# Placing the first pair of the next feed-forward quarter ahead of this quarter's second product, and beginning that product with its B11 block

## The chip, the cores and the metric

The kernel runs on one core of a Trainium2 chip. The metric is device time in microseconds (us) of the whole kernel, from launch to end, as the median of several runs. A profiled execution of the same program gives the trace; its own time is given beside its span.

The engines that matter here are TensorE (PE in the profile; PEld is its weight load), VectorE (DVE), ScalarE (ACT), GpSimd (POOL, which here issues the accumulating DMAs) and SyncE (SP, which issues the plain ones).

## What is computed

The reference is a decoder trunk of two layers on 512 tokens and 16 meta tokens, with a model width of 1024. Each layer runs a mixer of three head groups, a layer norm, a squared-ReLU feed-forward block of width 4096, and a second layer norm. Only the feed-forward block is touched by the change:

```python
def squared_relu_mlp(h, w1, w2):
    return jnp.square(jax.nn.relu(h @ w1)) @ w2
...
    for l in range(DEPTH):
        mix = hybrid_mixer(h, w_in[l], mla_q_norm[l], mla_kv_norm[l], w_uq[l], w_ukv[l], w_out[l], pos, valid)
        h = layer_norm(DN_ALPHA * h + mix, ln1_g[l], ln1_b[l])
        h = layer_norm(DN_ALPHA * h + squared_relu_mlp(h, w_ff1[l], w_ff2[l]), ln2_g[l], ln2_b[l])
```

## The kernel before

**Precision.** Every float32 operand is split into a high part and a low part, `hi` by a cast on ScalarE and `lo` by a subtraction on VectorE. Each product is three matmuls (hi·hi, hi·lo, lo·hi).

**Tiling.** Activations lie transposed, features on partitions and tokens along the free dimension. The feed-forward width of 4096 is cut into four quarters of 1024 (`qd` 0 to 3). In a quarter the first product (`h @ w1`, function `ff1_pair`) makes eight 128-row tiles, two at a time, as four pairs (`i` 0 to 3). The second product (`... @ w2`, function `ff2_pair`) reads that quarter's eight tiles and adds to the eight output tiles `r`, again two at a time, as four pairs (`m` 0 to 3). In quarter 0 three of the four pairs of the first product are made without the block scheme (`ff1`); in quarter 3 two of the four pairs of the second product are (`ff2`).

**Strassen pairs.** A pair is one step of Strassen's scheme in Winograd's form: `strassen` makes seven block products of half the tokens each (264 columns in layer 0, 256 in layer 1). They go by the names `x1` (A11 by B11), `z1` (S1 by T1), `z2` (S4 by B22), `x2` (S2 by T2), `y` (A12 by B21), `x3` (S3 by T3) and `x4` (A22 by T4). With four contraction tiles and three matmuls each, a block product has 12 matmuls and a pair 84. The products sum up in three PSUM banks: X collects x1, x2, x3 and x4, Z collects z1 and z2, Y holds y. After each product a function of the dictionary `done` reads the bank (in a second product: VectorE adds it to a half of `r`), and the next product into that bank has to wait for this read.

**What VectorE has to do.** A pair's weights come by five plain loads and two accumulating ones (`strassen_weights`). VectorE adds two sums and subtracts seven low parts, nine instructions of 512 columns. In a first-product pair it also makes the block sums B and T of the squared ReLU and their low parts: three instructions of 512 or 528 columns and eight of 256 or 264 (nine in quarter 3). In a second-product pair it does the seven additions to `r`, of 256 or 264 columns.

**Buffers.** The pools are `U` (75 tiles of 528 columns, activations), `W` (14 tiles, split weights, as many as one pair needs), `R` (8 tiles, raw weights) and 8 PSUM banks.

**What sets the order.** `record` writes every instruction down in program order, and `Recorder.schedule` (line 312) then puts them in order with a cost model of its own: each engine takes the instruction that can start first by the model, and of equals the one with the lower rank, then the one written first (lines 347 and 350). All pairs of a layer's feed-forward block have one rank (line 1418), so the order in which the loops call `ff1_pair` and `ff2_pair` decides among them. A matmul of a later pair is put ahead wherever the model sees the next product not ready. On the chip each engine then takes its own list strictly as it stands.

Of the kernel before, what the change touches and what calls it, by code (L numbers as in the profile page):

```python
# [225 lines left out]
class Recorder:  # L226
# [13 lines left out]
    def add(self, eng, fn, args, kw):  # L240
        op = Op()
        op.i, op.eng, op.fn, op.args, op.kw = len(self.ops), eng, fn, args, kw
        op.prio = (self.cur, op.i)
        ins, outs = [], []
        named = [("", a) for a in args] + list(kw.items())
        for n, (k, v) in enumerate(named):
            if isinstance(v, View):
                is_out = k in ("out", "accum_out") or (n == 0 and k == "")
                (outs if is_out else ins).append(v)
        deps = set()  # L250
        op.tiles = []
        for w, vs in ((False, ins), (True, outs)):
            for v in vs:
                box = v.box()
                t = v.t
                if t.cls.name == "ps":
                    box = (0, P, 0, 1 << 30)
                if t not in op.tiles:
                    op.tiles.append(t)
                keep = []  # L260
                for (o, ow, b) in t.hist:
                    hit = b[0] < box[1] and box[0] < b[1] and b[2] < box[3] and box[2] < b[3]
                    if hit and (w or ow) and o is not op:
                        deps.add(o)
                    covered = w and box[0] <= b[0] and b[1] <= box[1] and box[2] <= b[2] and b[3] <= box[3]
                    if not (covered and o is not op):
                        keep.append((o, ow, b))
                keep.append((op, w, box))
                t.hist = keep
        for t in op.tiles:  # L270
            t.left += 1
        op.deps = deps
        op.users = []
        self._cost(op, ins, outs)
        self.ops.append(op)
        return op
# [149 lines left out]
class Builder:  # L426
# [176 lines left out]
    def parts(self, d, H):  # L603
        def run(x, names, hi=None, lo=None):
            n = H * len(names)
            if hi is None:
                hi, lo = self.unit(F32R)[:, :n], self.unit(F32R)[:, :n]
            self.split(hi, lo, x[:, :n], "a")
            for j, k in enumerate(names):
                d[k] = (hi[:, j * H:j * H + H], lo[:, j * H:j * H + H])  # L610
            return hi, lo
        return run
# [734 lines left out]
    def layer(self, l, h, first):  # L1347
# [74 lines left out]
        H = NQ // 2  # L1422
        us, xs, hs = [[] for _ in range(4)], {}, []
# [15 lines left out]
        def ff1_pair(qd, i):  # L1439
            w = self.strassen_weights(self.a["wff1"][l, 8 * qd + i], self.a["wff1"][l, 8 * qd + i + 4])  # L1440
            z1 = self.unit()[:, :H]
            A, B = slice(0, H), slice(H, 2 * H)
            sub, stt = nc.vector.tensor_sub, nc.vector.scalar_tensor_tensor
            d = {}
            parts = self.parts(d, H)

            def square(x, scale, src):
                nc.scalar.activation(x, src, AF.Relu, scale=scale)
                nc.scalar.activation(x, x, AF.Square)


            p, q, t, m = (self.unit() for _ in range(4))
            b11, b12, b21, b22 = p[:, A], m[:, A], t[:, A], q[:, A]
            t1, t2, t3, t4 = p[:, B], m[:, B], q[:, B], t[:, B]
            if qd == 3:
                b12, b22, t1, t3 = p[:, B], t[:, B], m[:, A], q[:, B]
                t4 = q[:, A]
            if i % 2 == 0:
                self.half = [(self.unit(F32R), self.unit(F32R)) for _ in range(2 if qd == 3 else 1)]
            o = B if i % 2 else A  # L1460

            def x1(X, Y, Z):
                nc.vector.tensor_add(b11, X, b11)
                square(b11, 1.0, b11)

            def x2(X, Y, Z):
                nc.vector.tensor_add(b12, X, b12)
                square(b12, 1.0, b12)
                sub(t1, b11, b12)
                if qd == 3:  # L1470
                    parts(t1, ("t1",), *(x[:, o] for x in self.half[1]))
                    d["plain"] = [parts(p, ("b11", "b12"))]
                else:
                    parts(p, ("b11", "t1"))

            def x3(X, Y, Z):
                nc.vector.tensor_add(b22, X, z1)
                square(b22, -1.0, b22)
                sub(t3, b22, b12)
                stt(out=t2, in0=t3, scalar=-1.0, in1=b11, op0=ALU.mult, op1=ALU.subtract)  # L1480
                parts(t2, ("t2",), *(x[:, o] for x in self.half[0]))
                if qd < 3:
                    parts(q, ("b22", "t3"))

            def x4(X, Y, Z):
                square(b21, -1.0, X)
                stt(out=t4, in0=t2, scalar=-1.0, in1=b21, op0=ALU.mult, op1=ALU.subtract)
                if qd == 3:
                    d["plain"].append(parts(t, ("b21", "b22")))
                    parts(q, ("t4", "t3"))  # L1490
                else:
                    parts(t, ("b21", "t4"))
            self.strassen(w, hs, ("z1", "y", "x1", "z2", "x2", "x3", "x4"), H, dict(
                z1=lambda X, Y, Z: nc.scalar.copy(z1, Z), y=lambda X, Y, Z: nc.scalar.copy(b11, Y),
                z2=lambda X, Y, Z: nc.scalar.copy(b12, Z), x1=x1, x2=x2, x3=x3, x4=x4))
            us[qd].append(d)

        def ff2_pair(qd, m):
            w = self.strassen_weights(self.a["wff2"][l, qd, 2 * m], self.a["wff2"][l, qd, 2 * m + 1])

            def add(row, col, op=ALU.add):
                def run(ps):
                    mt, c = 2 * m + row, slice(col * H, col * H + H)
                    o = r[mt][:, c]
                    if (mt, col) not in touched:
                        touched.add((mt, col))
                        nc.vector.scalar_tensor_tensor(out=o, in0=o, scalar=ALPHA, in1=ps, op0=ALU.mult, op1=op)
                    else:
                        nc.vector.tensor_tensor(o, o, ps, op=op)
                return run  # L1510
            sub = ALU.subtract
            self.strassen(w, us[qd], ("z1", "x1", "z2", "x2", "y", "x3", "x4"), H, dict(
                z1=lambda X, Y, Z: add(1, 1, sub)(Z), x1=lambda X, Y, Z: add(0, 0)(X), z2=lambda X, Y, Z: add(0, 1)(Z),
                x2=lambda X, Y, Z: add(0, 1)(X), y=lambda X, Y, Z: add(0, 0)(Y), x3=lambda X, Y, Z: add(1, 1, sub)(X),
                x4=lambda X, Y, Z: add(1, 0, sub)(X)))

# [39 lines left out]
            us[0].append(self.strassen_inputs(xs[i][1][:, :NQ], xs[i + 4][1][:, :NQ], H, i))  # L1556
        for i in range(npl, 4):
            ff1_pair(0, i)
        for m in range(4):
            ff2_pair(0, m)  # L1560
        for qd in range(1, 4):
            for i in range(4):
                ff1_pair(qd, i)
            for m in range(4 if qd < 3 else 4 - nf // 2):
                ff2_pair(qd, m)
        plain = [u["plain"][0] for u in us[3]] + [u["plain"][1] for u in us[3]]
        final = l == DEPTH - 1
        ws = {mt: self.wload(self.a["wff2"][l, 3, mt]) for mt in range(8 - nf, 8)}
# [174 lines left out]
```

## Time and profile before

| | before |
|---|---|
| median of 3 runs | 1547.27 us (1546.6 to 1547.67) |
| the profiled execution's own time | 1546.99 us |
| its span | 1545.2 us |
| PE busy | 1504.6 us, 97% of the span |
| DVE busy | 1303.8 us, 84% |
| ACT busy | 963.7 us, 62% |
| share of the chain that ended last: PE, DVE, ACT | 87%, 9%, 2% |

The feed-forward blocks lie at about 480 to 770 us (layer 0) and 1229 to 1510 us (layer 1) of the span. All matmuls of a helper stand under one line of the program (L414), so stretches of time, not lines, tell the stages apart. A group of rows "PE ... x672" in the timeline is a run of matmuls without an idle gap between them; the bracket behind a row gives the idle time ahead of it and whose signal ended that time.

### The profile page before, as it was taken

The page shows a single profiled execution, that of the slowest core. Times are in us where ns is not written, and L with a number is a line of the kernel's source. Part 1 is how long each engine was busy: PE and PEld are TensorE (multiplying, and loading weights), DVE is VectorE, ACT ScalarE, POOL GpSimd, SP SyncE. Part 2 cuts the span into 40 slices and gives each one's busy share as a digit, 9 for nine tenths or more (in the row PEclk, how much of TensorE's full clock was granted, in tenths as well). Part 3 has the DMA queues.
Part 4 walks back from the last instruction along what each step waited for, and adds up shares of the span by engine and source line. Part 5 has one row for each costly group of instructions (what it writes and reads, how often), then busy time and mean ns, then how long its engine had stood idle before and what let it go on. Part 6 is the DMA issues. An engine that isn't in the chain of part 4 may idle for free.

```text
span 1545.2 us, 31629 instructions
## 1 busy us (share of the span) xinstructions
PE 1504.6 (97%) x11490; PEld 1443.6 (93%) x11490; DVE 1303.8 (84%) x3131; ACT 963.7 (62%) x2263; POOL 197.9 (13%) x309
## 2 busy tenths in 40 slices
PE   6999999999999999999999999999999999999997
PEld 6999999988999999999999999888889899999996
DVE  7778877998789898888877778779987988989896
ACT  5675744578667484757646657446884857666670
POOL 4113100010001111111102112001000011111110
PEclk9999999999999999999999999999999999999999
DMA  5424412321124767677514333424212277777752
GB/s 196 117 78 124 141 62 76 100 81 49 56 83 115 185 165 178 177 181 175 171 56 131 103 91 95 127 76 125 57 62 83 69 190 180 186 183 181 186 154 82
DMA packets 102668, 190.32 MB, mean 123 GB/s; under 512 B 13552, under 2 KB 14832, under 8 KB 102512
## 3 DMA queue, kind: packets, MB, share of 16 engines
q1 hardware_dynamic: 81840, 145.98, 30.0%
q0 software_dynamic: 20672, 42.32, 14.9%
q8 instruction: 90, 1.47, 0.4%
q14 instruction: 66, 0.54, 0.1%
HBM read 167.87 MB, written 2.10 MB: 110 GB/s over the span
## 4 chain that ended last, share of the span: by engine, by line
PE 87%; DVE 9%; ACT 2%; issue 1%; DMA 0%; SPq 0%; DVEq 0%; ACTq 0%
PE ps L414 87%; DVE u L414 6%; ACT u L414 2%; DVE t L414 2%; DVE w L414 1%; DMA u<-in_xm 0%; SPq L414 0%; DVE r L414 0%; ACT w L414 0%; DVEq L1738 0%; ACT t L414 0%; DVEq L414 0%; ACTq L414 0%
## 5 line engine op out<-in xcount | busy, mean ns | idle before, releaser
L414 PE MATMUL ps<-u,w 128*128 128x256 f32 (+3 forms) x9384 | 1281.2, 294 | 14.7 <-DVE u L414 7.6
L414 PEld LDWEIGHTS ps<-u,w 128*128 128x128 f32 x9384 | 1199.7, 189 | 49.7 <-DVE u L414 11.3
L414 ACT CAST w<-r 128x512 fp32r<-128x512 f32 x610 | 364.5, 617 | 293.0 <-PE ps L414 249.2
L414 DVE TENSOR_TENSOR w<-r,w 128x512 fp32r<-128x512 f32 x604 | 404.8, 686 | 59.2 <-ACT w L414 42.9
L414 DVE TENSOR_TENSOR u<-u,u 128x512 fp32r<-128x512 f32 (+10 forms) x541 | 283.3, 548 | 10.8 <-ACT u L414 8.9
L414 DVE TENSOR_TENSOR u<-ps,u 128x256 fp32r<-128x256 f32 (+11 forms) x518 | 198.0, 409 | 48.3 <-ACT u L414 28.8
L414 PE MATMUL ps<-u,u 128*128 128x272 f32 (+5 forms) x1012 | 183.8, 307 | 1.7 <-ACT u L414 0.9
L414 POOL DMA_DIRECT2D r<-in_wff x108 | 94.8, 881 | 652.0 <-DVE u L414 331.4
L414 ACT CAST u<-u 128x512 fp32r<-128x512 f32 (+7 forms) x287 | 149.8, 540 | 39.9 <-DVE u L414 34.7
L414 ACT ACTIVATE u<-u 128x256 f32<-128x256 f32 (+5 forms) x349 | 161.7, 475 | 15.3 <-DVE u L414 12.3
L414 PEld LDWEIGHTS ps<-u,u 128*128 128x128 f32 (+1 forms) x1012 | 150.2, 190 | 8.6 <-ACT u L414 1.4
L414 ACT ACTIVATE u<-ps 128x512 f32<-128x512 f32 (+9 forms) x185 | 88.6, 484 | 89.8 <-PE ps L414 78.6
L414 DVE TENSOR_TENSOR u<-u,ps 128x256 f32<-128x256 f32 (+3 forms) x236 | 98.7, 429 | 43.6 <-PE ps L414 42.3
L414 POOL DMA_DIRECT2D u<-u x112 | 58.0, 523 | 483.7 <-ACT u L414 442.6
L414 PE MATMUL ps<-ident,u 128*128 128x128 f32 x672 | 103.4, 278 | 12.4 <-DVE t L414 9.2
L414 ACT COPY u<-ps 128x256 f32<-128x256 f32 (+6 forms) x186 | 72.1, 395 | 54.3 <-PE ps L414 52.2
L414 PEld LDWEIGHTS ps<-ident,u 128*128 128x128 f32 x672 | 79.7, 142 | 19.1 <-DVE t L414 7.9
L414 ACT CAST u<-ps 128x16 fp32r<-128x16 f32 (+7 forms) x260 | 72.4, 330 | 26.4 <-PE ps L414 15.8
L414 DVE TENSOR_TENSOR r<-r,r 128x512 f32<-128x512 f32 x108 | 74.0, 685 | 2.3 <-DMA r<-in_wff 2.1
L414 DVE SCALAR_TENSOR_TENSOR u<-ps,u 128x512 f32<-128x512 f32 (+7 forms) x73 | 41.6, 579 | 25.5 <-ACT u L414 23.2
L414 ACT ACTIVATE u<-ps,t 128x512 f32<-128x512 f32 (+4 forms) x86 | 48.0, 561 | 16.7 <-DVE t L414 13.5
L414 DVE CAST u<-u 128x256 fp32r<-128x256 f32 (+5 forms) x147 | 49.6, 353 | 8.2 <-ACT u L414 7.7
(57 smaller groups left out, 600.6 us busy)
## 6 DMA issues: line engine op xcount, KB each, us to landing
r<-in_wff SPq DMA_DIRECT2D x310, 256.0 KB, 3.3
r<-in_win SPq DMA_DIRECT2D x120, 256.0 KB, 3.0
r<-in_wff POOLq DMA_DIRECT2D x108, 256.0 KB, 4.8
r<-in_wout SPq DMA_DIRECT2D x48, 256.0 KB, 2.9
u<-u POOLq DMA_DIRECT2D x80, 132.0 KB, 4.0
u<-u SPq DMA_DIRECT2D x48, 66.0 KB, 2.4
u<-in_xm SPq DMA_DIRECT2D x10, 256.0 KB, 5.5
u<-in_dec SPq DMA_DIRECT2D x8, 264.0 KB, 3.5
```

What stands on the lines that cost most here:

```text
L414: o.ins = getattr(getattr(nc, o.eng), o.fn)(*[r(x) for x in o.args], **{k: r(x) for k, x in o.kw.items()})
```

## The change

Two things change, both in `layer`. The loop over the quarters calls `ff1_pair(qd + 1, 0)` ahead of the second product of quarter `qd` (for `qd` 0 to 2), and the other three pairs of the next quarter after it. And a second-product pair's block products begin with x1, then z1, where they began with z1, then x1.

```diff
-            self.strassen(w, us[qd], ("z1", "x1", "z2", "x2", "y", "x3", "x4"), H, dict(
-                z1=lambda X, Y, Z: add(1, 1, sub)(Z), x1=lambda X, Y, Z: add(0, 0)(X), z2=lambda X, Y, Z: add(0, 1)(Z),
+            self.strassen(w, us[qd], ("x1", "z1", "z2", "x2", "y", "x3", "x4"), H, dict(
+                x1=lambda X, Y, Z: add(0, 0)(X), z1=lambda X, Y, Z: add(1, 1, sub)(Z), z2=lambda X, Y, Z: add(0, 1)(Z),
...
-        for m in range(4):
-            ff2_pair(0, m)
-        for qd in range(1, 4):
-            for i in range(4):
-                ff1_pair(qd, i)
+
+        for qd in range(4):
+            if qd < 3:
+                ff1_pair(qd + 1, 0)
             for m in range(4 if qd < 3 else 4 - nf // 2):
                 ff2_pair(qd, m)
+            for i in range(1, 4 if qd < 3 else 0):
+                ff1_pair(qd + 1, i)
```

The number of instructions on every engine is the same. The handover from quarter 1's first product to its second in layer 0 shows the move.

TensorE before, from the last matmuls of z1 and x1 that need the last first-product pair (banks ps_8682 and ps_8726), over two matmuls each of the following second-product pair (ps_8820, ps_8832) and one of y, to the first of z2:

```order
L414 MATMUL ps_8682<-u_8768,w_8643 128x264
L414 MATMUL ps_8682<-u_8784,w_8643 128x264
L414 MATMUL ps_8682<-u_8768,w_8655 128x264
L414 MATMUL ps_8726<-u_8768,w_8650 128x264
L414 MATMUL ps_8726<-u_8784,w_8650 128x264
L414 MATMUL ps_8726<-u_8768,w_8702 128x264
L414 MATMUL ps_8820<-u_8242,w_8815 128x264
L414 MATMUL ps_8820<-u_8256,w_8815 128x264
L414 MATMUL ps_8832<-u_8242,w_8825 128x264
L414 MATMUL ps_8832<-u_8256,w_8825 128x264
L414 MATMUL ps_8740<-u_8834,w_8723 128x264
L414 MATMUL ps_8682<-u_8298,w_8752 128x264
```

These rows follow directly on the last pair's x4.

TensorE in the changed kernel at the same place, from the end of that x4 (bank ps_8574): z2 and then x2 of the first pair of quarter 2 (banks ps_8682 and ps_8731), which read `h`:

```order
L414 MATMUL ps_8574<-u_7207,w_8614 128x264
L414 MATMUL ps_8574<-u_7192,w_8629 128x264
L414 MATMUL ps_8682<-u_6725,w_8757 128x264
L414 MATMUL ps_8682<-u_6712,w_8774 128x264
L414 MATMUL ps_8682<-u_6731,w_8757 128x264
L414 MATMUL ps_8682<-u_6740,w_8757 128x264
L414 MATMUL ps_8682<-u_6731,w_8774 128x264
L414 MATMUL ps_8682<-u_6736,w_8757 128x264
L414 MATMUL ps_8682<-u_6746,w_8757 128x264
L414 MATMUL ps_8682<-u_6736,w_8774 128x264
L414 MATMUL ps_8731<-u_7036,w_8700 128x264
L414 MATMUL ps_8731<-u_7045,w_8700 128x264
```

The second product's first matmul now stands 20 matmuls behind the x4, and its z2 stands 90 behind it, where it stood 11 behind.

VectorE before at this handover, from the last pair's T3 to the additions of z1 and x1 to `r` (u_6653 and u_6644), with weight parts (w, r) between:

```order
L414 TENSOR_TENSOR u_8771<-u_8771,u_8687 128x264
L414 TENSOR_TENSOR r_8799<-r_8760,r_8704 128x512
L414 SCALAR_TENSOR_TENSOR u_8687<-u_8771,u_8631 128x264
L414 TENSOR_TENSOR u_8813<-u_8771,u_8802 128x528
L414 TENSOR_TENSOR w_8818<-r_8576,w_8764 128x512
L414 TENSOR_TENSOR u_8690<-u_8687,u_8676 128x264
L414 SCALAR_TENSOR_TENSOR u_8811<-u_8687,u_8811 128x264
L414 TENSOR_TENSOR w_8830<-r_8598,w_8796 128x512
L414 TENSOR_TENSOR u_6653<-u_6653,ps_8682 128x264
L414 TENSOR_TENSOR u_8841<-u_8811,u_8834 128x528
L414 TENSOR_TENSOR u_6644<-u_6644,ps_8726 128x264
L414 TENSOR_TENSOR w_8851<-r_8620,w_8815 128x512
```

VectorE in the changed kernel, from the last pair's last low part (u_8919) to the first additions to `r`:

```order
L414 TENSOR_TENSOR u_8919<-u_8834,u_8901 128x528
L414 TENSOR_TENSOR w_8927<-r_8704,w_8892 128x512
L414 TENSOR_TENSOR u_8792<-u_8792,u_8868 128x264
L414 TENSOR_TENSOR u_8942<-ps_8731,u_8737 128x264
L414 TENSOR_TENSOR w_8950<-r_8753,w_8916 128x512
L414 TENSOR_TENSOR w_8960<-r_8776,w_8930 128x512
L414 TENSOR_TENSOR u_8970<-u_8792,u_8947 128x528
L414 TENSOR_TENSOR u_8942<-u_8942,u_8868 128x264
L414 TENSOR_TENSOR u_6644<-u_6644,ps_8874 128x264
L414 SCALAR_TENSOR_TENSOR u_8868<-u_8942,u_8792 128x264
L414 TENSOR_TENSOR u_6653<-u_6653,ps_8896 128x264
L414 TENSOR_TENSOR u_9004<-u_8942,u_8990 128x528
```

Between the two stand parts of the next quarter's first pair (u_8792, u_8942, u_8970) and more weight parts; before, the addition of z1 came ahead of the last low part.

## Rows read from the trace of the kernel before

**Rows 1.** The page: busy engines, the chain by engine, two kinds of DMA issue.

```profile
PE 1504.6 (97%) x11490; PEld 1443.6 (93%) x11490; DVE 1303.8 (84%) x3131; ACT 963.7 (62%) x2263; POOL 197.9 (13%) x309
...
PE 87%; DVE 9%; ACT 2%; issue 1%; DMA 0%; SPq 0%; DVEq 0%; ACTq 0%
...
r<-in_wff SPq DMA_DIRECT2D x310, 256.0 KB, 3.3
```

**Rows 2.** Busy time and instructions (x) of each engine in equal stretches.

```profile
core 0: us, PE busy (x) PEld busy (x) DVE busy (x) ACT busy (x) POOL busy (x), PEclk, DMA share, GB/s
484.00:500.00 16.00, 12.88 (x102) 12.24 (x101) 15.61 (x31) 11.26 (x24) 3.50 (x4) 1.00 0.70 174
512.00:528.00 16.00, 16.00 (x134) 16.00 (x133) 13.45 (x27) 6.85 (x12) 3.21 (x4) 1.00 0.69 180
576.00:592.00 16.00, 14.45 (x101) 13.72 (x100) 13.19 (x27) 7.95 (x17) 1.98 (x3) 0.89 0.57 162
664.00:680.00 16.00, 14.45 (x117) 14.02 (x115) 15.14 (x32) 8.63 (x17) 3.50 (x4) 1.00 0.68 172
746.00:762.00 16.00, 15.64 (x127) 15.22 (x126) 15.66 (x33) 9.15 (x19) 3.02 (x5) 1.00 0.61 177
1232.00:1252.00 20.00, 17.43 (x129) 16.62 (x128) 18.04 (x37) 12.91 (x29) 3.47 (x4) 0.91 0.68 166
1256.00:1276.00 20.00, 20.00 (x172) 20.00 (x171) 17.65 (x36) 9.18 (x16) 3.65 (x5) 1.00 0.77 205
1326.00:1346.00 20.00, 19.34 (x158) 18.60 (x157) 18.85 (x40) 10.13 (x19) 3.50 (x4) 1.00 0.79 201
1407.00:1427.00 20.00, 19.29 (x157) 18.54 (x156) 18.86 (x40) 10.16 (x19) 3.50 (x4) 1.00 0.80 198
1480.00:1500.00 20.00, 19.14 (x155) 18.25 (x154) 19.97 (x41) 14.97 (x33) 1.76 (x3) 1.00 0.63 164
```

**Rows 3.** Timeline of PE alone, layer 0: start, duration, what; idle ahead.

```profile
485.37 1.73 PE L414 MATMUL ps<-u,w 128*128 128x264 f32 x12 [0.99 <-ACT w L414]
488.33 8.22 PE L414 MATMUL ps<-u,w 128*128 128x264 f32 x65 [1.24 <-DVE u L414]
497.44 82.04 PE L414 MATMUL ps<-u,w 128*128 128x264 f32 x672 [0.89 <-DVE u L414]
580.00 0.51 PE L414 MATMUL ps<-u,w 128*128 128x264 f32 x2 [0.52 <-ACT w L414]
581.14 0.51 PE L414 MATMUL ps<-u,w 128*128 128x264 f32 x2 [0.64 <-ACT w L414]
582.05 83.48 PE L414 MATMUL ps<-u,w 128*128 128x264 f32 x668 [0.40 <-ACT u L414]
667.07 85.16 PE L414 MATMUL ps<-u,w 128*128 128x264 f32 x691 [1.54 <-ACT w L414]
```

**Rows 4.** Timeline of PE alone, layer 1.

```profile
1237.57 9.46 PE L414 MATMUL ps<-u,w 128*128 128x256 f32 x65 [2.00 <-DVE u L414]
1247.30 1.91 PE L414 MATMUL ps<-u,w 128*128 128x256 f32 x14 [0.28 <-DVE u L414]
1249.51 77.86 PE L414 MATMUL ps<-u,w 128*128 128x256 f32 x658 [0.29 <-DVE u L414]
```

**Rows 5.** The stretches behind two of these waits, columns as in Rows 2.

```profile
582.30:585.60 3.30, 3.30 (x16) 3.27 (x16) 1.98 (x4) 0.22 (x1) 0.21 (x1) 0.50 0.51 173
1237.70:1241.00 3.30, 3.30 (x16) 3.30 (x17) 2.72 (x6) 1.85 (x5) 0.00 (x0) 0.50 0.90 259
```

**Rows 6.** Timeline of DVE alone, ahead of the wait at 1237.57 and at 501.

```profile
1235.29 1.89 DVE L414 TENSOR_TENSOR w<-r,w 128x512 fp32r<-128x512 f32 x3
1237.09 0.42 DVE L414 TENSOR_TENSOR u<-ps,u 128x256 f32<-128x256 f32 x1
1237.43 0.68 DVE L414 TENSOR_TENSOR w<-r,w 128x512 fp32r<-128x512 f32 x1
...
501.36 0.76 DVE L414 TENSOR_TENSOR u<-u,ps 128x264 f32<-128x264 f32 x2
```

## The prediction, made before the changed kernel ran

> **What bounds the kernel now.** I read the page first, for which engine to follow: TensorE is busy 97% of the span and carries 87% of the chain that ended last; VectorE is second with 84% busy and 9% of the chain [rows 1]. So time is gained only where TensorE stands still. Then I read equal stretches across the two feed-forward blocks and counted matmuls. A lossless 16 us in layer 0 holds 134, a lossless 20 us in layer 1 holds 172; the stretches over the handovers from a quarter's first product to its second hold fewer [rows 2]. One matmul takes 82.04 / 672 = 0.122 us in layer 0 [rows 3] and 77.86 / 658 = 0.118 us in layer 1 [rows 4], so each missing matmul is worth that much. Lost per handover:
>
> - layer 0: quarter 0, 134 - 102 = 32 matmuls, 3.9 us; quarter 1, 33, 4.0 us; quarter 2, 17, 2.1 us; quarter 3, 7, 0.85 us
> - layer 1: quarter 0, 172 - 129 = 43, 5.1 us; quarter 1, 14, 1.65 us; quarter 2, 15, 1.8 us; quarter 3, 17, 2.0 us
>
> Together 21.4 us. Between the handovers runs of some 670 matmuls stand without an idle gap [rows 3, 4], so nothing else in these blocks can be won.
>
> Last I read the timeline of TensorE for what it waits for. At 580.00, 581.14 and 582.05 it runs two matmuls, waits, runs two more and waits again [rows 3]: the work that the scheduler put in as a filler is itself not ready. Behind the second of these waits and behind the one of 2.00 us at 1237.57, the granted clock is 0.50, which is the lower level of 1.2 GHz, and 3.30 us hold 16 matmuls [rows 5]. Half of that time is lost, 1.65 us each; it is contained in the 4.0 and the 5.1.
>
> **Why TensorE waits there.** VectorE runs its list without a pause in these stretches (15.61 of 16 us, 19.97 of 20 [rows 2]). Three weight subtractions in a row take 1.89 us, two steps and one duration of 0.68, so a long instruction costs a step of 0.605 us; two short ones take 0.76, a step of 0.34 [rows 6]. A first-product pair has 12 long and 8 short: 7.26 + 2.72 = 10.0 us, against 84 matmuls or 10.25 us in layer 0 and 9.9 in layer 1. A second-product pair has 9 and 7: 7.8 us. So VectorE has no reserve in the first product, and the last pair's results are due at once when the second product begins.
>
> I can put that into a balance: start where the last pair's x2 begins, just released by VectorE's read of x1, and count what VectorE must finish before some product, and the matmuls ahead of that product in TensorE's order. Before, for z2 of quarter 1 in layer 0: 66 matmuls, 8.05 us, against 12 long and 10 short, 10.65 us; short by 2.6, and 4.0 - 1.65 = 2.35 were lost. Quarter 2: short by 2.4, lost 2.1. Layer 1, quarters 1 and 2: 71 matmuls against 11 and 10, short by 1.7 each, lost 1.65 and 1.8. Quarter 3 of layer 1: 72 against 13 and 9, short by 2.4, lost 2.0. Quarter 0: short by 0.5 and 0.8, lost 1.15 in either layer after its first waits (below). Only quarter 3 of layer 0 is off, short by 2.5 with 0.85 lost. The balance is good to about half a microsecond.
>
> **The change, part by part.**
>
> *The move.* Ten us of matmuls of the next quarter's first pair, which need only `h`, now lie between the last pair and the second product. Freed are the handovers of quarters 1 and 2: 4.0 + 2.1 + 1.65 + 1.8 = 9.55 us.
>
> Of quarter 0 only a part is freed. The engines' lists up to the last pair's x2 keep their order, with the moved pair's weights in the place of the second product's, so the waits at 485.37 and 488.33 stay, and so does the one at 1237.57 with its half-clock stretch. In layer 0 the three idle times sum to 3.12 us of 3.9 lost, so a restart costs 0.26 besides; kept are 0.99 + 1.24 + 0.52 = 2.75, freed 1.15. In layer 1 idle is 2.57, half clock 1.65, and 0.29 remain per restart; kept are 2.00 + 1.65 + 0.29 = 3.95, freed 1.15. Quarter 0 frees 2.3 us; with the others 11.85.
>
> *New waits.* The same balance on the changed order. Its tightest places: layer 0, quarter 0, 104 matmuls (12.7 us) against 16 long and 8 short (12.4), spare 0.3; quarter 1 spare 0.2 (30 matmuls against 4 and 3); quarter 2 spare 0.2. Layer 1: quarter 0 spare 0.2, quarter 1 spare 0.1; quarter 2 short by 1.0 (156 matmuls, 18.4 us, against 22 and 18, 19.4 us). Nothing is comfortable: VectorE and TensorE run level for two pairs instead of one running dry. Where the spare is 0.1 to 0.3 and the method is good to half a microsecond, I take 0.3 us lost for each of the five, 1.5, and 1.0 for the sixth: 2.5 us. Bounds: 0, if every spare holds, and 5 x 0.5 + 1.5 = 4.0.
>
> *Quarter 3* has no next quarter to borrow from, but its order changes too: with x1 first, x2 can stand ahead of z2, and x2 needs T2, ready before the plain low parts for z2. Short by 0.25 in layer 0 (69 matmuls against 11 and 6) and by 0.75 in layer 1 (57 against 9 and 6), where 0.85 and 2.0 are lost now. I take 0.25 and 0.75: 1.85 us won; the bounds are 2.85 and nothing.
>
> *Swapping x1 and z1.* z2 adds to the bank that VectorE reads after z1, and now follows z1 at once in program order. In the built order at least 9 matmuls (1.1 us) stand between two products of one bank, as in most pairs of before, where runs of 670 show no gap [rows 3]. No cost; were that cover gone, a read's step and its queue, 0.3 to 0.7 us, in each of 28 pairs.
>
> *The moved loads.* The pair's seven DMAs (five on SyncE, two on GpSimd) now go ahead of 20 and 8 of the four second-product pairs. A load lands in 3.3 us [rows 1], no wait of TensorE in rows 3 and 4 is for one, and the raw-weight pool keeps eight under way. Nothing. *Held tiles:* the moved pair's results, 8 units (10 in quarter 3), stay through the second product. With 8 of `r`, 28 of `h` and its sums and 28 of the quarter, 64 were held; 74 of 75 at most now, plus temporaries. It fits, and late takers show in the order; I put the 1.0 us of quarter 2 in layer 1 partly down to that.
>
> **Sum.** 11.85 + 1.85 - 2.5 = 11.2 us. The profiled execution took 1546.99 us, 0.28 under the median: 1546.99 - 11.2 + 0.28 = 1536.1, call it **1536**.
>
> **The rivals.**
>
> *A, more is won.* The spares hold, and the stretch at half clock behind 1237.57 does not come, as none came behind 1.54 us at 667.07 [rows 3]: 2.5 + 1.65 more, 1532. Against it: the wait of 2.00 stays, and both stretches followed about 2 us of standing.
>
> *B, VectorE's queue in order.* At 1235.29 three weight subtractions, 1.89 us, stood ahead of the short read that TensorE needed, and TensorE stood for 2.00 [rows 4, 6]. The changed order mixes two pairs' parts at six handovers. One such inversion in three of them costs 5.7 us and gives 1541.5; in all six 11.3, giving 1547, no change. For it: no spare absorbs 1.89. Against it: the built order keeps 9 matmuls between bank and read, and the steady first product ran as tight without loss. The Trainium skill, "PSUM — Partial Sum Buffer", section "Engine vs sequencer instructions", says that VectorE's queue is a strict FIFO; by that rule a read placed late holds TensorE however short it is, and the rows at 1235.29 agree.
>
> *C, slower.* The same inversion, each followed by a half-clock stretch, as at 1237.57: 1.89 + 1.65 = 3.5 us per handover, six times 21 us in place of the 2.5 taken: 1536 + 21 - 2.5 = 1554.5. The median passes 1547.3 from four such handovers (14 us), and a measured slowdown needs five. Against it: today two of eight have such a stretch, and both follow the longest waits.
>
> *D, nothing moves,* the scheduler undoing the loop's order: 1547. The built order speaks against it.
>
> **How the numbers follow.** Forecast 0.68 (1533.5 to 1540); A 0.10; B in half 0.09, in full 0.07; C 0.05; D 0.01. The range 1532 to 1542 takes in the forecast, A and half of B: 0.87. A measurement of this kernel tells about 0.2%, 3.1 us, from no change, so below 1544.2 is faster: 0.68 + 0.10 + 0.09 = 0.87; same 0.08; slower 0.05.
>
> **What the changed profile would show.** Right: matmul counts over the handovers of quarters 1 and 2 near 132 in 16 us and 169 in 20; full clock behind what was 580; the waits at 485, 488 and near 1237 still there, the two after the last and the one at 497 gone; quarter 3 of layer 1 above 155. Wrong: pairs of short runs with idle for DVE inside the interleaved stretch, or half-clock stretches there. The sum is wrong if VectorE's steps get longer, or if the second product's later pairs, lossless now, show gaps.

## The result, and the profile after

The changed kernel takes 1535.17 us (median, 1533.81 to 1536.25) against 1546.93 for the kernel before on the same chip: a ratio of 0.9925, 95% interval 0.9911 to 0.9938. The forecast was 1536.0. The profiled execution took 1534.93 us with a span of 1533.2, so 12.06 us less than the profiled execution of before.

Busy shares say little: PE is at 98% of the span, VectorE at 85%, ScalarE at 63%, one point more each than in [rows 1]. The gain shows in TensorE's timeline. Layer 0, after (start, duration, what, then the idle time ahead and who ended it; these two rows answer to [rows 3]):

```profile
485.26 1.72 PE L414 MATMUL ps<-u,w 128*128 128x264 f32 x12 [0.99 <-ACT w L414]
488.23 277.04 PE L414 MATMUL ps<-u,w 128*128 128x264 f32 x2272 [1.25 <-DVE u L414]
```

Layer 1, after; the first row answers to the wait at 1237.57 in [rows 4]:

```profile
1229.38 49.72 PE L414 MATMUL ps<-u,w 128*128 128x256 f32 x403 [1.99 <-DVE u L414]
1279.64 129.93 PE L414 MATMUL ps<-u,w 128*128 128x256 f32 x1097 [0.55 <-DVE u L414]
1410.44 79.52 PE L414 MATMUL ps<-u,w 128*128 128x256 f32 x670 [0.87 <-DVE u L414]
```

In layer 0 one run of 2272 matmuls stands from 488 to 765 us (the window of this view ends there) without an idle gap, over three handovers at which TensorE stood before. In layer 1 three waits are left, where before there were nine. The equal stretches over the handovers, columns as in [rows 2], and a last one behind the wait at 1229.38:

```profile
484.00:500.00 16.00, 13.76 (x111) 13.33 (x110) 15.74 (x31) 11.60 (x28) 3.49 (x4) 1.00 0.71 185
576.00:592.00 16.00, 16.00 (x134) 16.00 (x133) 15.56 (x33) 13.32 (x32) 3.49 (x4) 1.00 0.80 183
664.00:680.00 16.00, 16.00 (x133) 16.00 (x133) 15.75 (x33) 12.00 (x25) 1.75 (x2) 1.00 0.62 152
746.00:762.00 16.00, 16.00 (x135) 16.00 (x134) 12.92 (x27) 5.86 (x11) 0.00 (x0) 1.00 0.57 185
1222.00:1242.00 20.00, 18.01 (x138) 17.65 (x137) 18.48 (x37) 14.57 (x35) 3.46 (x4) 0.91 0.70 177
1256.00:1276.00 20.00, 19.97 (x169) 19.77 (x169) 19.06 (x38) 8.72 (x16) 3.49 (x4) 1.00 0.85 212
1326.00:1346.00 20.00, 20.00 (x171) 20.00 (x170) 19.64 (x42) 11.11 (x23) 3.49 (x4) 1.00 0.72 175
1407.00:1427.00 20.00, 19.13 (x162) 18.93 (x162) 19.38 (x40) 10.32 (x20) 3.50 (x4) 1.00 0.76 192
1480.00:1500.00 20.00, 20.00 (x172) 20.00 (x171) 16.76 (x34) 8.74 (x16) 0.00 (x0) 1.00 0.36 105
1230.20:1233.50 3.30, 3.30 (x18) 3.30 (x17) 3.13 (x6) 1.57 (x4) 0.52 (x1) 0.50 0.87 258
```

A lossless stretch holds 134 (layer 0) or 172 (layer 1). At 576, 664, 746, 1326 and 1480 nothing or next to nothing is lost now. The stretch at 576 has full clock, where it was at 0.89. What is left: 23 matmuls at 484 (2.8 us), 34 at 1222 (4.0 us, half clock among it), 10 at 1407 (1.2 us), 3 at 1256 (0.35 us), and the wait at 1279.64 (0.55 idle, 0.7 with its restart). That is about 9.0 of the 21.4 us lost before, so 12.4 us were won by this count and 12.06 by the profiled times.

### The profile page after: what moved, and what is told of

It reads as the page before. It is cut to its first block, busy times and chain, and to the rows that moved or that the text cites. A ratio compares the mean times of both kernels' runs of the same rounds, so it can differ in the third digit from the quotient of the medians.

```text
span 1533.2 us, 31621 instructions
## 1 busy us (share of the span) xinstructions
PE 1497.7 (98%) x11490; PEld 1440.9 (94%) x11490; DVE 1301.6 (85%) x3131; ACT 963.7 (63%) x2263; POOL 197.4 (13%) x309
## 4 chain that ended last, share of the span: by engine, by line
PE 86%; DVE 10%; ACT 1%; issue 1%; DMA 1%; DVEq 0%; SPq 0%; POOLq 0%; ACTq 0%
PE ps L414 86%; DVE u L414 6%; DVE t L414 2%; DVE w L414 2%; ACT u L414 1%; DMA r<-in_wff 1%; DVE r L414 0%; DMA u<-in_xm 0%; DVEq L1739 0%; ACT t L414 0%; DVEq L414 0%; SPq L414 0%; POOLq L414 0%; ACTq L414 0%
## 5 line engine op out<-in xcount | busy, mean ns | idle before, releaser
L414 DVE TENSOR_TENSOR u<-u,u 128x512 fp32r<-128x512 f32 (+10 forms) x541 | 283.7, 548 | 11.8 <-ACT u L414 9.8
```

The source lines that it names most:

```text
L414: o.ins = getattr(getattr(nc, o.eng), o.fn)(*[r(x) for x in o.args], **{k: r(x) for k, x in o.kw.items()})
```

## The experiments

All times below are medians. "Before" is the kernel before, run beside each on the same chip: 1545.53 us for the first four, 1546.03 for the next four, 1545.09 for the last three. Line numbers in the edits are left out; diffs are against the changed kernel unless said otherwise.

### One part at a time

*The move alone*, with the old order of block products:

```diff
-            self.strassen(w, us[qd], ("x1", "z1", "z2", "x2", "y", "x3", "x4"), H, dict(
+            self.strassen(w, us[qd], ("z1", "x1", "z2", "x2", "y", "x3", "x4"), H, dict(
```

> The loop change alone; the second product's block products begin with z1, as before. Theory (the moved pair gives VectorE the time that it lacked, the swap only helps quarter 3): the handovers of quarters 0 to 2 lose as little as in the changed kernel, at most 1 us each; quarter 3, whose order now puts z2 ahead of x2 again, loses 2.0 us (layer 0) and 2 to 4 us (layer 1) by the balance of VectorE's instructions, where the changed kernel loses nearly nothing: 1540 us (1537 to 1541). Rival (the swap carries the gain at the handovers): near 1545.

Measured 1540.03 us, ratio 0.9959 (0.9945 to 0.9974). In its profile the handovers of quarters 1 and 2 are about as free as in the full change (134, 129, 172 and 169 matmuls in the stretches at 576, 664, 1326 and 1407), and quarter 3 loses. Windows of this kernel over quarter 3 of both layers:

```profile
740.00:756.00 16.00, 15.22 (x123) 14.91 (x123) 15.41 (x32) 8.47 (x17) 2.48 (x4) 1.00 0.61 181
1478.00:1498.00 20.00, 18.56 (x150) 17.95 (x151) 16.85 (x34) 8.70 (x16) 0.00 (x0) 1.00 0.42 119
```

11 and 22 matmuls are missing, 1.3 and 2.6 us, which the full change doesn't lose. The five runs of this kernel spread from 1535.73 to 1541.8 us, and the profile is of the fastest: it lies only 0.8 us above the changed kernel's, since it has no half-clock stretch and loses less around 1279 and 1407. What the other four runs lost besides, no trace shows.

*The swap alone*, with the old loop:

```diff
-        for qd in range(4):
-            if qd < 3:
-                ff1_pair(qd + 1, 0)
+        for m in range(4):
+            ff2_pair(0, m)
+        for qd in range(1, 4):
+            for i in range(4):
+                ff1_pair(qd, i)
...
-            for i in range(1, 4 if qd < 3 else 0):
-                ff1_pair(qd + 1, i)
```

> The swap alone, x1 ahead of z1, with the loops as before. Theory: the handovers of quarters 1 and 2 keep their waits, by the balance 2.9 and 1.3 us (layer 0) and 1.7 and 1.7 us (layer 1), with a stretch at half clock behind the first; quarter 3 short by 1.6 and 1.8 us: 1545 us (1543 to 1547). Rival (the swap carries the gain): 1537.

Measured 1542.7 us, ratio 0.998 (0.997 to 0.9989), just below the range expected. Windows of this kernel over the handovers of quarters 1, 2 and 3, first layer 0, then layer 1:

```profile
574.00:590.00 16.00, 15.21 (x123) 14.79 (x122) 15.60 (x33) 11.27 (x23) 1.86 (x3) 1.00 0.69 175
656.00:672.00 16.00, 16.00 (x131) 15.84 (x131) 15.71 (x33) 11.81 (x25) 1.75 (x2) 1.00 0.67 163
740.00:756.00 16.00, 15.17 (x121) 14.69 (x121) 15.59 (x33) 10.72 (x23) 2.47 (x4) 1.00 0.55 152
1319.00:1339.00 20.00, 19.35 (x158) 18.61 (x157) 19.75 (x41) 11.06 (x22) 3.49 (x4) 1.00 0.71 173
1400.00:1420.00 20.00, 19.32 (x158) 18.58 (x157) 19.83 (x41) 11.08 (x22) 3.49 (x4) 1.00 0.74 180
1476.00:1496.00 20.00, 19.12 (x155) 18.24 (x154) 20.00 (x43) 14.39 (x32) 1.75 (x2) 1.00 0.64 166
```

In layer 1 the handovers of quarters 1 and 2 lose what they lost before (158 of 172 each; before 158 and 157). In layer 0 they don't: 11 and 3 matmuls are missing where 33 and 17 were, so there the expectation failed, and the swap alone takes most of these two waits away; why it does so in layer 0 only was not tried. Quarter 3 is not helped (13 and 17 missing; before 7 and 17). And neither of the two half-clock stretches of the kernel before is in this profile, which is part of the gain.

By the medians the swap alone is worth 2.8 us, the move alone 5.5, both together 11.8. The move frees quarters 1 and 2 of both layers and leaves quarter 3 worse off; the swap alone does nothing for quarter 3; only the two together free it.

### Is it the order of VectorE's list, or how much stands in it?

Two waits stay in the changed kernel, at 488.23 and 1229.38, each ended by one short read of VectorE. The rows ahead of the second (VectorE, changed kernel) look like an inversion, an urgent read behind work that can wait:

```profile
1225.57 1.62 DVE L414 TENSOR_TENSOR u<-u,u 128x512 fp32r<-128x512 f32 x3
1227.11 1.88 DVE L414 TENSOR_TENSOR w<-r,w 128x512 fp32r<-128x512 f32 x3
1228.91 0.41 DVE L414 TENSOR_TENSOR u<-ps,u 128x256 f32<-128x256 f32 x1
```

*Two low parts to GpSimd.* `strassen_weights` marks the subtractions for S3 and A22, and after scheduling the marked ones change engine:

```diff
+        self.mark = mark
         w["s3"] = self.wsplit(t["s3"])
         w["a22"] = self.wsplit(t["a22"])
...
+        for o in self.pooled:
+            o.eng = "gpsimd"
```

First in the last pair of quarter 0, with the changed kernel's order:

> The changed kernel with its order kept as it is, but the low parts of S3 and A22 of the pair (quarter 0, i 3) are subtracted by GpSimd in place of VectorE; these are two of the three weight subtractions that stood ahead of the read of x1 for which TensorE waits near 488 and 1229. Theory (the read is late by what stands ahead of it in VectorE's list, and the half-clock stretch follows the wait): the wait at 488 of 1.25 us goes to under 0.3, the one at 1229 from 1.99 to about 0.8, and the stretch at half clock behind it goes: 1.2 + 1.2 + 1.65 = 4 us, so 1531. Rival (the read waits for the chain of products itself, not for VectorE's list): 1535, with both waits as they are.

Measured 1535.79 us: no change. Then in the first second-product pair of quarters 1 to 3, with the order of the kernel before:

> The kernel before with its order kept, but the low parts of S3 and A22 of the first second-product pair of quarters 1 to 3 are subtracted by GpSimd: two long instructions, 1.21 us, less in VectorE's list between the last first-product pair's x1 and z2's release at each of six handovers. Theory (VectorE's throughput sets the wait): each of the six shrinks by about 1.2 us or to nothing, and the half-clock stretch near 582 goes: 8 us less in all, 1539. Rival (the wait is the latency of the chain read, square, sum, low part, whatever else VectorE does): 1547.

Measured 1560.63 us, ratio 1.0093, slower where 1539 was expected. VectorE of the first of these kernels, at the place:

```profile
486.82 3.73 DVE L414 TENSOR_TENSOR w<-r,w 128x512 fp32r<-128x512 f32 x2
```

and GpSimd beside it:

```profile
486.55 2.84 POOL L414 TENSOR_TENSOR w<-r,w 128x512 fp32r<-128x512 f32 x2
```

VectorE of the second kernel, while GpSimd ran its two subtractions there:

```profile
579.90 3.20 DVE L414 SCALAR_TENSOR_TENSOR u<-u,u 128x264 f32<-128x264 f32 x1
```

Two VectorE steps that take 1.28 elsewhere took 3.73 us while GpSimd ran its two, and a short one of 0.42 took 3.20. VectorE was not relieved but stopped. So neither run says anything on the order or the load; they show a lock (last section).

*The same relief by ScalarE*, the kernel before with copies by ScalarE in the place of those subtractions, which this kernel leaves out:

```diff
+        for o in self.pooled:
+            o.eng, o.fn, o.args = "scalar", "copy", o.args[:2]
```

> The kernel before, and in the first second-product pair of quarters 1 to 3 of both layers the low parts of S3 and A22 are copies made by ScalarE instead of subtractions by VectorE: twelve VectorE steps of 0.6 less in all, GpSimd has none of them, and the subtraction itself is left out. Theory (at these handovers VectorE's number of steps sets the wait, as the doubled steps showed from the other side, and the earlier trial failed only because GpSimd's operation stopped VectorE): the six handovers lose 0.6 to 1.2 less each, 1538 to 1543 where the kernel before has 1546. Rival (the handover is bound by the chain from square to copy to next product, so steps of VectorE that stand beside it cost nothing): 1545 to 1548; ScalarE's twelve steps of 0.62 could cost as much again, which would show as waits for ScalarE.

Measured 1553.87 us, ratio 1.0056 (1.0043 to 1.0068): slower, the last clause of the expectation. TensorE of this kernel at the handover of quarter 1:

```profile
581.86 0.51 PE L414 MATMUL ps<-u,w 128*128 128x264 f32 x2 [1.16 <-ACT w L414]
```

ScalarE and VectorE there:

```profile
580.36 0.62 ACT L414 CAST w<-r 128x512 fp32r<-128x512 f32 x1
580.88 0.42 ACT L414 ACTIVATE u<-u 128x264 f32<-128x264 f32 x1
581.33 0.43 DVE L414 SCALAR_TENSOR_TENSOR u<-u,u 128x264 f32<-128x264 f32 x1 [0.41 <-ACT u L414]
```

and the same square and step in the kernel before:

```profile
580.16 0.42 ACT L414 ACTIVATE u<-u 128x264 f32<-128x264 f32 x1
580.91 0.42 DVE L414 SCALAR_TENSOR_TENSOR u<-u,u 128x264 f32<-128x264 f32 x1
```

The wait at 581.14 in [rows 3] was 0.64 and is now 1.16. VectorE did not wait at this step before; now it waits for a square of ScalarE, ahead of which a copy of 0.62 stands. The last squares of a quarter go from one engine to the other and back, so a step added on ScalarE's side of this chain delays it as well. Part of the 9 us is clock: the profile has four half-clock stretches, where that of the kernel before has two.

*The read put first in the list*, by moving VectorE's later-needed steps behind it, once per layer, without adding or dropping a step:

```diff
-        order = self.nc.schedule()
+        order = self.early(self.nc.schedule())
...
+    def early(self, order):
+        for read, n, keep in self.hoist:
+            i = order.index(read)
+            late = [o for o in order[:i] if o.eng == "vector"][-n:]
+            late = [o for o in late if o not in keep]
+            order = [o for o in order[:i] if o not in late] + [read] + late + order[i + 1:]
+        return order
```

> The changed kernel, with one alteration on VectorE's list alone, once per layer: in the last pair of quarter 0 the read of the second product of the bank (the one that PE waits for at 488.23 and 1229.38 of the changed kernel) stands right behind the low parts that the next products need; the low parts of S3 and A22 and those of the neighbouring squares, which PE needs only later, stand behind it. No step is added or dropped. Theory (these two waits are an order inversion on VectorE's list, nothing else): the waits of 1.25 and 1.99 go to under 0.3 each and nothing later grows by as much; the half-clock stretch after 1229, which the profile of the changed kernel had, does not come; 1531 to 1533 where the changed kernel has 1535.2. Rival (VectorE has too much to do there, so that what is let pass is late next): the same time as the changed kernel, 1534.5 to 1536, with new waits behind the two places that add up to what was won.

and in a second kernel at two more places:

> As e9, and at two more places of layer 1 a read goes ahead of the two or three VectorE steps before it: the read of the second product of the fourth second-product pair of quarter 0 (PE's wait of 0.71 at 1279.64 in the changed kernel), ahead of a weight sum that waits for its transfer and one low part; and the first read of the first second-product pair of quarter 2 (1.02 at 1410.44), ahead of one low part and two steps of the next quarter's squares. Theory: the swap's shorter distance to the next product is what made the wait at 1279.64, and an earlier read takes it away: both waits go to under 0.3 and the time lies 1 to 1.7 below that of e9, at 1529.5 to 1532. Rival: within 0.5 of e9, since the steps let pass are late in their turn.

Measured 1534.43 us (ratio 0.9932, 0.9918 to 0.9945) and 1533.55 us (0.9925, 0.9913 to 0.9938): the changed kernel's time. TensorE of the first, in both layers:

```profile
485.45 3.18 PE L414 MATMUL ps<-u,w 128*128 128x264 f32 x24 [0.99 <-ACT w L414]
489.02 279.46 PE L414 MATMUL ps<-u,w 128*128 128x264 f32 x2288 [0.39 <-DVE w L414]
...
1230.00 176.65 PE L414 MATMUL ps<-u,w 128*128 128x256 f32 x1488 [1.34 <-DVE w L414]
```

and of the second at 1410 of the changed kernel:

```profile
1409.53 78.25 PE L414 MATMUL ps<-u,w 128*128 128x256 f32 x659 [0.70 <-DVE u L414]
```

The waits for the reads are gone (x2 follows at once, one run of 24 matmuls). A product later TensorE waits for a low part of the next weights: 0.39 for 1.25, and 1.34 for 1.99. At 1410 the wait passed from the read of x1 to that of z1. The theory fell and the rival was right in the main: VectorE is behind with its work there. A better order takes back 0.86 and 0.65 us of idle time at the two waits, too little to tell from the changed kernel in the medians. The wait at 1279.64 is absent even in the first of the two, which didn't touch it, and the second has one of 0.58 at 642.35 in layer 0, where the two have the same list: waits of this size come and go.

### Two steps more

Here the marked low parts are done twice (the same result written again), so that VectorE has 1.2 us more work at a place:

```diff
+        order = [o for o in order for _ in range(2 if o in self.twice else 1)]
```

*In the moved pairs of the changed kernel*, six places:

> The changed kernel with its order kept, but in the six moved pairs (first pair of quarters 1 to 3) VectorE does the low parts of S3 and A22 twice: 1.21 us more in its list at each handover. Theory (VectorE and TensorE run level there, with a spare of 0.1 to 0.3 us and none in layer 1's quarter 2): each handover loses about 1.0 to 1.2 us, 6 us in all, 1541. Rival (the moved pair's 10 us of matmuls cover far more than was missing, so that there is reserve): 1535 to 1536.

Measured 1541.4 us, ratio 0.997 (0.996 to 0.998): 6 us more, as the theory had it. In layer 0 the doubled steps stand at 492 to 496, 577 to 581 and 660 to 664; windows over them, columns as in [rows 2]:

```profile
488.00:504.00 16.00, 15.39 (x120) 14.79 (x121) 15.89 (x31) 13.13 (x31) 2.62 (x3) 1.00 0.81 189
576.00:592.00 16.00, 15.84 (x130) 15.63 (x130) 15.93 (x33) 13.93 (x32) 2.63 (x4) 1.00 0.68 170
656.00:672.00 16.00, 15.75 (x127) 15.36 (x126) 15.72 (x31) 13.53 (x32) 1.74 (x2) 1.00 0.64 154
```

The changed kernel has 129, 134 and 133 in these windows. Over the three places of layer 1 (16 us from 1238, 1320 and 1398) it is 131, 131 and 130, where the changed kernel has 137 to 139 at the same places, 4 to 8 us earlier in its trace. That is 41 matmuls, 4.9 us, at the six places, 0.5 to 1.1 us each. The rest lies elsewhere, for instance here, TensorE and VectorE of this kernel:

```profile
532.33 53.67 PE L414 MATMUL ps<-u,w 128*128 128x264 f32 x436 [0.69 <-DVE u L414]
528.15 0.69 DVE L414 TENSOR_TENSOR w<-r,w 128x512 fp32r<-128x512 f32 x1 [1.39 <-ACT w L414]
```

This wait is not arrears that VectorE carries on: 4 us earlier VectorE itself had stood 1.39 us, waiting for a copy of ScalarE.

*In the third pair of the second product*, far from any handover:

> The changed kernel with its order kept, but in the third second-product pair of quarters 0 to 2 VectorE does the low parts of S3 and A22 twice, the same 1.21 us in six places. Theory (a second-product pair needs 7.8 us of VectorE against 10 us of matmuls, so there is reserve): nothing, or up to 0.3 us in places where such a subtraction lands ahead of a bank's read with 9 matmuls to cover it: 1535 to 1537. Rival (VectorE is the bound all through the interleaved order): 1541 or more.

Measured 1538.38 us, ratio 0.9952 (0.9937 to 0.9967): 3 us more, above the expectation. TensorE in layer 0:

```profile
557.14 54.58 PE L414 MATMUL ps<-u,w 128*128 128x264 f32 x446 [0.83 <-DVE u L414]
612.36 80.47 PE L414 MATMUL ps<-u,w 128*128 128x264 f32 x658 [0.64 <-DVE u L414]
693.63 6.57 PE L414 MATMUL ps<-u,w 128*128 128x264 f32 x52 [0.81 <-DVE u L414]
```

VectorE ahead of the first two of these waits:

```profile
555.43 0.69 DVE L414 TENSOR_TENSOR r<-r,r 128x512 f32<-128x512 f32 x1 [1.69 <-DMA r<-in_wff]
607.59 2.74 DVE L414 TENSOR_TENSOR w<-r,w 128x512 fp32r<-128x512 f32 x4
```

The doubled steps stand at 523 to 526, 607 to 610 and 690 to 693. At the second and the third place four low parts in a row, 2.74 us, delay a read, and TensorE waits 0.64 and 0.81. VectorE has spare time over the whole pair, and still single reads come late. The wait at 557.14 is of another kind: 30 us behind the doubled steps a weight sum stood 1.69 us waiting for its transfer.

*At the handovers of the kernel before*, first second-product pair of quarters 1 to 3:

> The kernel before with its order kept, but the low parts of S3 and A22 of the first second-product pair of quarters 1 to 3 are done twice by VectorE: 1.21 us more at each of six handovers. Theory (VectorE's throughput): each wait grows by 1.2 us, 7.3 in all, and the longer waits in quarters 2 and 3 bring one to three more stretches at half clock (1.65 us each): 1556 to 1559. Rival (latency of the chain): 1547 to 1548.

Measured 1562.06 us, ratio 1.0105 (1.0088 to 1.0121): the direction of the theory, and more than its size. Two of the stretches behind the longer waits, columns as in [rows 2]:

```profile
584.80:588.10 3.30, 3.30 (x18) 3.30 (x17) 2.21 (x6) 0.00 (x0) 0.82 (x1) 0.50 0.47 148
670.20:676.80 6.60, 6.23 (x27) 5.92 (x28) 4.20 (x9) 1.23 (x3) 0.87 (x1) 0.50 0.54 121
```

Five handovers now have half clock behind them, seven stretches of 3.41 us or 23.9 in sum, where the kernel before had two, 6.8. In the kernel with two low parts on GpSimd 5.00 us at half clock hold 24 matmuls (from 585) and 5.00 at full clock 44 (from 591), so 45% of such time is lost: 7.7 us of the difference. The rest of the 16 us measured, 8.3, is left for the longer waits themselves and their restarts, against the 7.2 of twelve steps of 0.6.

### Two pairs moved

```diff
                 ff1_pair(qd + 1, 0)
+                ff1_pair(qd + 1, 1)
...
-            for i in range(1, 4 if qd < 3 else 0):
+            for i in range(2, 4 if qd < 3 else 0):
```

> The changed kernel with two pairs of the next quarter ahead of the second product in place of one. Theory (one pair already frees all that can be freed there; the rest is VectorE running level and late tiles): no further gain; 8 more units of the activation pool are held, so the second pair's late results have to wait for tiles of the second product, and by the balance quarter 2 is short by 0.8 and 1.3 us: 1535 to 1539. Rival (the handovers are still limited by what can be put ahead): 1532 or less.

Measured 1547.77 us, ratio 1.0011: the whole gain is gone. TensorE in layer 1:

```profile
1459.62 0.50 PE L414 MATMUL ps<-u,w 128*128 128x256 f32 x2 [1.02 <-ACT w L414]
1460.84 24.56 PE L414 MATMUL ps<-u,w 128*128 128x256 f32 x206 [0.72 <-DVE u L414]
```

New waits of 0.2 to 1.0 us stand throughout both blocks; seven waits of this kernel, 5.4 us, are for a high part from ScalarE, where the changed kernel has one (1.0 us). All idle time of TensorE together is 5.1 us more than in the changed kernel, of the 11.4 between the two profiles' spans; the rest was not traced further. Whether ScalarE is late because the activation pool is full or because of where its copies stand was not tried, since the pool has no room to grow; it stays open.

## Why the prediction was right, point by point

**What bounds the kernel.** Right: time was to be won only where TensorE stood still, and by the counts above the gain came out of the handovers that were counted. One reading was a little off: of a half-clock stretch not half is lost but 45% (24 matmuls against 44, above), so 1.5 us and not 1.65. Rival B's price is also added up slightly wrong, 5.7 us on 1536 being 1541.7 and not 1541.5; no bound hangs on either.

**The move.** Quarters 1 and 2 were forecast to free 9.55 us; they have 134, 133 and 171 of 134 and 172, and 1.2 us left at 1407, which the sum had set apart as a new wait. The waits kept in quarter 0 were forecast at 2.75 and 3.95 and measured 2.8 and 4.0. The wait at 497 and the two behind 1237 are gone, as said. The move alone frees these handovers too, as the forecast had it; but in layer 0 the swap alone takes most of them away as well (11 and 3 matmuls missing for 33 and 17), which the forecast did not see. That the kept half-clock stretch came in this profile is in part luck, as the last section shows.

**New waits.** 2.5 us were taken, 1.0 of them in quarter 2 of layer 1. That one came, 10 matmuls or 1.2 us at 1407. Of the five at 0.3 none came in layer 0 (a run of 2272 without a gap); with 0.35 at 1256 and 0.7 at 1279.64 the total is 2.25. The size was right, its spread was not; that the parts balanced is luck.

**Quarter 3.** The term that was mis-sized: 1.85 us taken as won, both losses closed, 2.85, the upper bound. The balance saw 0.25 and 0.75 short where nothing is lost; the move alone shows that without the swap quarter 3 loses 1.3 and 2.6 us. But the reason given, that with x1 first x2 can stand ahead of z2, is not enough: with the swap alone 13 and 17 matmuls are missing there, 1.6 and 2.0 us. What the move adds at this handover was not tried.

**"Swapping x1 and z1: no cost", "the moved loads: nothing."** Not quite. At 1279.64 VectorE, in the changed kernel:

```profile
1277.92 0.69 DVE L414 TENSOR_TENSOR r<-r,r 128x512 f32<-128x512 f32 x1 [1.09 <-DMA r<-in_wff]
1278.57 0.69 DVE L414 TENSOR_TENSOR w<-r,w 128x512 fp32r<-128x512 f32 x1
1279.18 0.41 DVE L414 SCALAR_TENSOR_TENSOR u<-u,ps 128x256 f32<-128x256 f32 x1
```

A weight sum stood 1.09 us waiting for its transfer, and behind it the read of z1, whose bank z2 needed 11 matmuls on. On the page the sums' waits for a transfer grew from 2.1 to 4.8 us. This is rival B's mechanism in one place at 0.7 us, instead of 1.89 in three. In the kernel with the reads first the same sum did not wait, though nothing was altered near it.

**VectorE as the cause.** Half right. Two more steps cost time wherever they were put (3 to 16 us), at the handovers 0.5 to 1.1 us each in the changed kernel and 8.3 for six in the kernel before, and with the reads first the waits come back at the next weights: the amount of VectorE's work binds, not its order alone. But "VectorE has no reserve" left out ScalarE: twelve steps given to it cost 9 us. The handover is a chain through both engines, and what relieves it is work for TensorE that needs neither's latest results. Why a balance of VectorE's steps alone still met most sizes within half a microsecond stays open: the two engines are not equally loaded there (VectorE 13.19 and ScalarE 7.95 of 16 us at 576 in [rows 2]), and no run here tells the two shares of the chain apart.

**The rivals.** A's first half came for the spares in layer 0; its clock half did not come in this profile, but did in those of other kernels with the same wait (last section). C and D did not come.

## What to carry to other kernels

Where one product reads what the product before has just finished, count the matmuls between the last result and its first reader against the steps that the other engines still have to do; matmuls of the next stage that need only old data, put there, free the handover without making any engine faster. One pair was enough and two gave everything back, so move as much as the balance asks for and look at the waits again. An urgent read behind less urgent work is worth putting first only if its engine has spare time right behind: otherwise the wait moves to the next thing that is late.

## What the runs showed of the hardware

**GpSimd stops VectorE.** While GpSimd ran two subtractions of 512 columns with both inputs in SBUF (2.84 us for the two), one VectorE instruction stood for the whole of them: 3.20 us in place of 0.42, and two took 3.73 in place of 1.28. The Trainium skill, "SBUF — State Buffer", section "Who interferes with whom", says that a VectorE instruction with two SBUF inputs contends with a GpSimd instruction that reads SBUF, and that issue order decides who blocks. The traces agree on the contention. On the order they don't tell: VectorE stood both where its recorded start comes after GpSimd's (486.82 and 486.55) and where it comes before (579.90 and 579.98). The price here was nearly GpSimd's whole span, not one of its instructions.

**The same wait, with and without half clock.** Behind a wait of 1.98 to 2.00 us near 1230 to 1245 the granted clock fell to 0.50 (the level of 1.2 GHz) for 3.41 us in some executions and stayed at 1.00 in others. The kernel with the move alone, in its profile, right behind this wait (columns as in [rows 2]; the changed kernel's row is the last of its windows above):

```profile
1230.80:1234.10 3.30, 3.30 (x29) 3.30 (x30) 3.30 (x7) 2.53 (x7) 0.41 (x1) 1.00 0.77 229
```

29 matmuls against 18 in 3.30 us. Of the ten profiles with this wait five had the stretch (the kernel before, the changed one, the two with low parts on GpSimd or ScalarE at the handovers of before, and the one with doubled steps in the moved pairs), and five had not (the move alone, the swap alone, two pairs moved, and the other two with doubled steps). The kernel before and the one with doubled steps at its handovers have the same instructions around this wait, and only the first had the stretch. So about 1.5 us of a single profile's time can be there or not.
